# A decoder trunk in split float32: the residual weights' slots moved by 64 bytes, with longer slots and a smaller transfer scratch

## The chip, the cores and the metric

The kernel runs on one core of a Trainium2 chip. A core has a matmul engine (TensorE, PE in the profile; its loads of stationary operands are listed as PEld), VectorE (DVE), ScalarE (ACT), GpSimd (POOL) and SyncE (SP), which issues most transfers between HBM and SBUF, the on-chip memory of 128 partitions. Matmul results go to PSUM banks. The metric is the device time of one execution in microseconds (us); lower is better.

## The reference, cut to what matters

The trunk has two layers on 256 positions of width 2048. Each layer has a token mixer (forgetting attention in the first, sliding-window attention in the second) and a gated feed-forward block with a short convolution; all operands are float32.

```python
for i in range(DEPTH):
    mod = c_act @ ada_w[i] + ada_b[i]
    sh1, sc1, g1, sh2, sc2, g2 = jnp.split(mod[:, None, :], 6, axis=-1)
    h = x * (1.0 + sc1) + sh1
    ...
    x = layer_norm(DEEPNORM_ALPHA * x + (1.0 + g1) * y, ln_mix_g[i], ln_mix_b[i])
    h = x * (1.0 + sc2) + sh2
    y = conv_ffn(h, ffn_w_up[i], ffn_conv_w[i], ffn_conv_b[i], ffn_w_down[i])
    x = layer_norm(DEEPNORM_ALPHA * x + (1.0 + g2) * y, ln_ffn_g[i], ln_ffn_b[i])
```

The mixers' projections, the up projection (2048 to 11264) and the down projection (5632 to 2048) are the large products. Weights are read once each, 256 positions wide.

## The kernel before, in words

**Split operands.** TensorE multiplies in the type float32r, a rounded float32. To keep precision, each operand is split in two: a rounded part (h, "high") and a residual (l, "low"), which is the operand minus its rounded part. A product is then three matmuls: high by high, high by low, low by high. For weights the function `stream` does this, a block at a time: a transfer (L261) brings 256 rows by 512 columns of a weight matrix into a slot `w` as 128 partitions x 2 x 512 elements, ScalarE rounds it into `wh` (L264), and VectorE subtracts, `wl = w - wh` (L275, in `residual_`, which is placed in the program some steps ahead of use). Then `go` runs the matmuls that use the pair. There are 728 such blocks.

**Three ways to use a block.** In `w_mm` (outputs named ws in the profile) and `u_mm` (us) a 128 x 128 slice of the weights is the stationary operand and the activations `hHL` are streamed; hHL holds for each block of 128 features 256 high and then 256 low elements. `u_mm`, the up projection, alternates: stationary slice of wh, 512 columns streamed (high and low together); stationary slice of wl, 256 columns streamed (high alone). `w_mm` uses 256 columns each: wh with high, wh with low, wl with high. In `x_mm` (outputs xs) it is the other way about: the activations are stationary, 128 positions at a time, and 512 columns of wh or wl are streamed, in the order wh by high, wl by high, wh by low. The stationary operand is then hHL (value projection of the first mixer, projections of the second), `oT` (attention output, in both output projections; the last four of its sixteen blocks are kept in hHL's place) or `gT` (down projection). All these matmuls are recorded at L75, in the helper `mm`. A stationary operand is loaded while the matmul before it still streams, as the starts in the PEld rows show.

**Memory.** Tiles come from pools of slots of equal length, one set for each tag; a slot starts at a multiple of 32 bytes. `wp` has ten slots of 4,096 bytes (tag w, also used for the modulation weights wa and others), `hl` four slots for wh and four for wl, each of 4,096 bytes, and `gp` thirty slots of 2,048 bytes (gT, oT, and others). In front of all pools lies a scratch for transfers issued by POOL, 4,096 bytes a partition, set in `kernel` (L1179). In the allocation of the program a partition has, from its first byte on:

```text
scratch        0     hHL      27904     w (10 slots)   78816
x           6912     acc      62080     wh (4 slots)  119776
                                        wl (4 slots)  136160
                                        gp (30 slots) 152544
                                        end           229256
```

Modulo 128 this makes 0 for hHL and 96 for w, wh, wl and gp, in every slot.

**Order.** The tile framework orders instructions and places the waits. SP issues the transfers of weights (w and wa), in program order. POOL issues small ones: rows of parameters (L146 to L175) and the bias row of a gate (L392), 1 MB broadcast to all partitions. VectorE also accumulates the modulation vectors (L404), one step of which `tick` adds after each block. Between sublayers the layer norm runs: moments on VectorE (L636 to L641), the power of -1/2 on POOL (L642), normalising on ScalarE and VectorE (L652, L654), transposes on TensorE (L493) and the split into hHL.

Of the kernel before, what the change touches and what calls it, by code (L numbers as in the profile page):

```python
# [11 lines left out]
F32R = mybir.dt.float32r  # L12
# [5 lines left out]
P = 128  # L18
# [18 lines left out]
WB = 512  # L37
# [4 lines left out]
def hybrid_trunk(ctx: ExitStack, tc: tile.TileContext, a: dict, out: bass.AP):  # L42
    nc = tc.nc
# [6 lines left out]
    hl = ctx.enter_context(tc.tile_pool(name="hl", bufs=4))  # L50
# [4 lines left out]

    def wtile(name="w"):
        return wp.tile([P, 2, WB], F32, tag="w", name=name)

    def gtile(name="g"):
        return gp.tile([P, 2, S], F32R, tag="g", name=name)  # L60
# [16 lines left out]
    def pin(ins, on=True):  # L77

        if on:
            tc.keep_in_program_order(ins)  # L80
# [140 lines left out]
    def settle(left=0):  # L221
        while work and (ahead[0] > left or not left):
            f = work.pop(0)
            rest(f, *work)
            f()
# [21 lines left out]
    def run_post():  # L247
        for g in list(post):
            if next(g, post) is post:
                post.remove(g)  # L250
# [5 lines left out]
    def stream(wsrc, row0, col, ks, use):  # L256

        for kc in ks[::2]:
            r0 = (row0 + kc) * P
            w = wtile()  # L260
            pin(nc.sync.dma_start(w, wsrc[r0:r0 + 2 * P, col:col + WB].rearrange("(k p) f -> p k f", p=P)), False)  # L261
            h = hl.tile([P, 2, WB], F32R, tag="wh", name="wh")
            l = hl.tile([P, 2, WB], F32R, tag="wl", name="wl")
            pin(nc.scalar.copy(h, w), False)  # L264

            def go(kc=kc, h=h, l=l):
                ahead[0] -= 1
                run_post()
                use(kc, h, l)
                if feeds:  # L270
                    feeds.pop(0)()
                tick()

            def residual_(w=w, h=h, l=l, go=go):
                pin(nc.vector.tensor_tensor(l, w, f32(h), op=ALU.subtract), behind[0] > 0)  # L275
                behind[0] -= 1
                del residuals[go]

            ahead[0] += 1
            weights.add(go)  # L280
            residuals[go] = residual_
            work.append(go)
            settle(2)
# [46 lines left out]
    def x_stationary(wsrc, col, k0, nk, stat, end=0):  # L330

        ps = x_banks()
        use = x_mm_end(ps, stat, nk, end) if end else lambda kc, h, l: x_mm(ps, kc, h, l, stat, nk - 1)
        stream(wsrc, k0, col, list(range(nk)), use)
        return ps

    def w_stationary(wsrc, col):

        ps = u_banks()
        stream(wsrc, 0, col, list(range(KC)), lambda kc, h, l: u_mm(ps, kc, h, l))  # L340
        return ps
# [24 lines left out]
    def tick():  # L366
        ada_tick()
        if not feeds:
            step()
# [10 lines left out]
    def ada_vector(l, v):  # L380
# [14 lines left out]
        for k in range(KC):  # L395
            for c in range(0, D, D // 2):
                w = wtile("wa").rearrange("p a f -> p (a f)")
                pin(nc.sync.dma_start(w, a["ada_w"][l, k * P:(k + 1) * P, v * D + c:v * D + c + D // 2]), False)
                for o in range(0, D // 2, step_):
                    ac, wo = part(c + o, step_), w[:, o:o + step_]  # L400
                    if k == 0 and not row:
                        pin(nc.vector.tensor_scalar_mul(ac, wo, cact[:, 0:1]), True)
                    else:
                        pin(nc.vector.scalar_tensor_tensor(ac, wo, (cactp if row else cact)[:, k:k + 1], ac,  # L404
                                                           op0=ALU.mult, op1=ALU.add), True)
                yield
# [249 lines left out]
    def ln_rows(name, l):  # L656
        gb, bb = [], []
        for c in range(0, D, D // 2):
            for b, nm in ((gb, "_g"), (bb, "_b")):
                w = wtile("ln")  # L660
                nc.sync.dma_start(w.rearrange("p a f -> p (a f)"), a[name + nm][l, c:c + D // 2].partition_broadcast(P))
                b += [w[:, 0, :], w[:, 1, :]]
        return gb, bb
# [78 lines left out]
    def out_proj(oT, full, w_o, l):  # L742
        def stat(kc, t):
            while kc not in full:
                step()
            return oT[kc][0][:, t * P:(t + 1) * P], oT[kc][1][:, t * P:(t + 1) * P]

        ps = {d: x_banks() for d in range(2)}

        def part(d, ks):  # L750
            use = x_mm_end(ps[d], stat, KC, 2) if d == D // WB - 1 else                 lambda kc, h, l_: x_mm(ps[d], kc, h, l_, stat, KC - 1)
            stream(w_o, 0, d * WB, ks, use)

        for i, ks in enumerate((range(0, 8), range(8, 12))):
            then(lambda i=i: ada.update(rate=((1.3, 1.3, 1.3, 1.3), (0.9,) * 4)[l][i]))
            for d in range(2):
                part(d, list(ks))
        then(lambda: ada_need(l, 2))
        for d in range(D // WB):
            if d < 2:  # L760
                part(d, list(range(12, KC)))
            else:
                then(lambda d=d: ada.update(rate=((1.3, 1.3, 1.3, 1.3), (0.9,) * 4)[l][d]))
                ps[d] = x_banks()
                part(d, list(range(KC)))
            then(lambda d=d: defer(residual(ps[d], d, gates[l, 2], True)), d == D // WB - 1)
        then(lambda: (flush(), ada.update(gate_free=True)), True)
# [423 lines left out]
```

## Time and profile before

| | |
|---|---|
| median of 3 runs | 2251.49 us (2250.17 to 2252.9) |
| the profiled execution | 2256.46 us |
| its span, first to last instruction | 2254.7 us |
| mean granted TensorE clock | 0.990 |
| matmuls | 12087 |
| moved from and to HBM | 602.66 MB |

A row of a group names line, engine, operation, output tile and inputs, shapes and a count, then the group's busy time, the mean duration of one in ns, and the idle time of the engine just before its instructions, with what ended it. The duration of a matmul includes its way through the array, so one that follows on the heels of another overlaps it: the distance from start to start is shorter than the duration. In a timeline row the first two numbers are start and length in us; neighbouring instructions of one form are merged, with their count behind the x.

### The profile page before, as it was taken

The page shows a single profiled execution, that of the slowest core. Times are in us where ns is not written, and L with a number is a line of the kernel's source. Part 1 is how long each engine was busy: PE and PEld are TensorE (multiplying, and loading weights), DVE is VectorE, ACT ScalarE, POOL GpSimd, SP SyncE. Part 2 cuts the span into 40 slices and gives each one's busy share as a digit, 9 for nine tenths or more (in the row PEclk, how much of TensorE's full clock was granted, in tenths as well). Part 3 has the DMA queues.
Part 4 walks back from the last instruction along what each step waited for, and adds up shares of the span by engine and source line. Part 5 has one row for each costly group of instructions (what it writes and reads, how often), then busy time and mean ns, then how long its engine had stood idle before and what let it go on. Part 6 is the DMA issues. An engine that isn't in the chain of part 4 may idle for free. (4 is left out here: it accounts for less than half of the span.)

```text
span 2254.7 us, 33120 instructions
## 1 busy us (share of the span) xinstructions
PE 2203.7 (98%) x12087; PEld 1908.6 (85%) x12087; DVE 1847.5 (82%) x2626; ACT 1209.7 (54%) x2009; POOL 22.8 (1%) x52
## 2 busy tenths in 40 slices
PE   6999999999999999999999999999999999999997
PEld 5999888788888888888887788788888888888886
DVE  6879999979989978799888899769988655676766
ACT  3435655455555543655634588746555533555542
POOL 0000000000000000000000000000000000000000
PEclk9999999999999999999999999999999999999999
DMA  9999999958978989889887777557887555565553
GB/s 336 371 336 364 349 357 325 329 200 298 327 266 296 315 299 339 272 277 319 280 309 284 244 246 243 206 185 262 289 270 256 190 192 195 189 193 189 188 195 112
DMA packets 274228, 602.66 MB, mean 267 GB/s; under 512 B 21062, under 2 KB 29960, under 8 KB 273552
## 3 DMA queue, kind: packets, MB, share of 16 engines
q1 hardware_dynamic: 273008, 595.85, 76.5%
q0 software_dynamic: 1056, 4.69, 0.6%
q8 instruction: 94, 1.54, 0.3%
q14 instruction: 70, 0.57, 0.1%
HBM read 598.37 MB, written 2.10 MB: 266 GB/s over the span
## 5 line engine op out<-in xcount | busy, mean ns | idle before, releaser
L264 ACT CAST wh<-w 128x1024 fp32r<-128x1024 f32 x728 | 763.8, 1051 | 806.4 <-PE us L75 284.5
L275 DVE TENSOR_TENSOR wl<-w,wh 128x1024 fp32r<-128x1024 f32 x728 | 887.2, 1223 | 297.0 <-ACT wh L264 285.1
L75 PE MATMUL us<-hHL,wh 128*128 128x512 f32 x2816 | 983.7, 393 | 0.0
L75 PE MATMUL us<-hHL,wl 128*128 128x256 f32 x2816 | 790.4, 282 | 3.0 <-DVE wl L275 3.0
L75 PEld LDWEIGHTS us<-hHL,wh 128*128 128x128 f32 x2816 | 528.9, 188 | 112.0 <-issue 2.5
L75 PEld LDWEIGHTS us<-hHL,wl 128*128 128x128 f32 x2816 | 533.0, 189 | 8.4 <-DVE wl L275 4.3
L75 PE MATMUL xs<-wh,gT 128*128 128x512 f32 x1408 | 435.5, 390 | 0.0
L75 PEld LDWEIGHTS xs<-wh,gT 128*128 128x128 f32 x1408 | 264.3, 188 | 54.6
L75 PE MATMUL xs<-wl,gT 128*128 128x512 f32 x704 | 273.9, 389 | 0.0
L75 PE MATMUL xs<-wh,hHL 128*128 128x512 f32 x704 | 237.6, 403 | 0.1
L404 DVE SCALAR_TENSOR_TENSOR acc<-wa,cact,acc 128x1024 f32<-128x1024 f32 x180 | 228.8, 1280 | 0.0
L75 PE MATMUL ws<-hHL,wh 128*128 128x256 f32 x1024 | 191.3, 289 | 4.4 <-ACT hHL L84 2.1
L75 PEld LDWEIGHTS ws<-hHL,wh 128*128 128x128 f32 x1024 | 163.1, 196 | 6.9 <-ACT hHL L84 2.3
L404 DVE SCALAR_TENSOR_TENSOR acc<-wa,cactp,acc 128x1024 f32<-128x1024 f32 x128 | 162.6, 1281 | 0.0
L75 PEld LDWEIGHTS xs<-wh,hHL 128*128 128x128 f32 x704 | 131.5, 189 | 29.4 <-issue 1.0
L75 PEld LDWEIGHTS xs<-wl,gT 128*128 128x128 f32 x704 | 132.2, 188 | 27.3
L75 PE MATMUL ws<-hHL,wl 128*128 128x256 f32 x512 | 144.7, 290 | 2.2 <-DVE wl L275 2.2
L75 PE MATMUL xs<-wl,hHL 128*128 128x512 f32 x352 | 140.6, 400 | 1.6 <-DVE wl L275 1.5
L75 PE MATMUL xs<-wh,oT 128*128 128x512 f32 x384 | 124.6, 394 | 0.8 <-ACT wh L264 0.7
L1075 ACT ACTIVATE u<-us,ccol 128x256 f32<-128x256 f32 x176 | 98.0, 561 | 39.6 <-DVE us L1073 39.5
L75 PEld LDWEIGHTS ws<-hHL,wl 128*128 128x128 f32 x512 | 99.5, 197 | 2.8 <-DVE wl L275 2.8
L1076 DVE SCALAR_TENSOR_TENSOR u<-us,ccol,u 128x255 f32<-128x255 f32 x176 | 83.6, 480 | 13.2 <-ACT u L1075 12.9
(222 smaller groups left out, 1761.2 us busy)
## 6 DMA issues: line engine op xcount, KB each, us to landing
w<-in_ffn_w_up_dram SPq DMA_DIRECT2D x352, 512.0 KB, 4.6
wa<-in_ada_w_dram SPq DMA_DIRECT2D x320, 512.0 KB, 5.4
w<-in_ffn_w_down_dram SPq DMA_DIRECT2D x176, 512.0 KB, 4.1
w<-in_fox_w_in_dram SPq DMA_DIRECT2D x96, 512.0 KB, 7.0
wo<-in_ada_w_dram SPq DMA_DIRECT2D x48, 512.0 KB, 8.4
w<-in_swa_w_in_dram SPq DMA_DIRECT2D x40, 512.0 KB, 5.0
w<-in_fox_w_o_dram SPq DMA_DIRECT2D x32, 512.0 KB, 6.2
w<-in_swa_w_o_dram SPq DMA_DIRECT2D x32, 512.0 KB, 4.7
```

Of the source, the lines that this page charges most:

```text
L75: return nc.tensor.matmul(o, lhsT, rhs, start=start, stop=stop, **kw)
L264: pin(nc.scalar.copy(h, w), False)
L275: pin(nc.vector.tensor_tensor(l, w, f32(h), op=ALU.subtract), behind[0] > 0)
L404: pin(nc.vector.scalar_tensor_tensor(ac, wo, (cactp if row else cact)[:, k:k + 1], ac, op0=ALU.mult, op1=ALU.add), True)
L1075: nc.scalar.activation(u, pf, AF.Identity, bias=cw(CW, f), scale=cw(2, f))
L1076: nc.vector.scalar_tensor_tensor(u[:, 1:], pf[:, :S - 1], cw(1, f), u[:, 1:], op0=ALU.mult, op1=ALU.add)
```

## The change

The slots of wh and wl become 128 bytes longer (32 elements), 4,224 in place of 4,096 bytes. The tile wh starts at the beginning of its slot as before, wl 64 bytes (16 elements) into its slot. The scratch for POOL's transfers becomes 2,048 in place of 4,096 bytes. No instruction is named, added or taken away by the diff.

```diff
+    def htile(name):
+        o = 16 * (name == "wl")
+        return hl.tile([P, 2 * WB + 32], F32R, tag=name, name=name)[:, o:o + 2 * WB].rearrange("p (k f) -> p k f", f=WB)
...
-            h = hl.tile([P, 2, WB], F32R, tag="wh", name="wh")
-            l = hl.tile([P, 2, WB], F32R, tag="wl", name="wl")
+            h, l = htile("wh"), htile("wl")
...
-    nc = _bacc.Bacc("TRN2", target_bir_lowering=False, num_devices=1, dynamic_dma_scratch_size=4096)
+    nc = _bacc.Bacc("TRN2", target_bir_lowering=False, num_devices=1, dynamic_dma_scratch_size=2048)
```

## The prediction

> **What bounds the kernel now.** I read the page first: busy times, then the clock row.
>
> ```profile
> span 2254.7 us, 33120 instructions
> PE 2203.7 (98%) x12087; PEld 1908.6 (85%) x12087; DVE 1847.5 (82%) x2626; ACT 1209.7 (54%) x2009; POOL 22.8 (1%) x52
> PEclk9999999999999999999999999999999999999999
> ```
>
> TensorE is without a matmul for only 2254.7 - 2203.7 = 51 us, at a granted clock of 0.9 or more in every slice. A busy matmul engine can still run slower than it might, so the question is how far apart matmuls start. The second view is the page's costliest groups:
>
> ```profile
> L264 ACT CAST wh<-w 128x1024 fp32r<-128x1024 f32 x728 | 763.8, 1051 | 806.4 <-PE us L75 284.5
> L275 DVE TENSOR_TENSOR wl<-w,wh 128x1024 fp32r<-128x1024 f32 x728 | 887.2, 1223 | 297.0 <-ACT wh L264 285.1
> L75 PE MATMUL us<-hHL,wh 128*128 128x512 f32 x2816 | 983.7, 393 | 0.0
> L75 PE MATMUL us<-hHL,wl 128*128 128x256 f32 x2816 | 790.4, 282 | 3.0 <-DVE wl L275 3.0
> ...
> L75 PE MATMUL xs<-wl,gT 128*128 128x512 f32 x704 | 273.9, 389 | 0.0
> ...
> L75 PE MATMUL ws<-hHL,wl 128*128 128x256 f32 x512 | 144.7, 290 | 2.2 <-DVE wl L275 2.2
> L75 PE MATMUL xs<-wl,hHL 128*128 128x512 f32 x352 | 140.6, 400 | 1.6 <-DVE wl L275 1.5
> ```
>
> The rounding on ScalarE (L264) waits mostly for TensorE to free a slot, and the subtraction on VectorE (L275) waits mostly for ScalarE: both are ahead of the matmuls. The list of TensorE's waits says the same. All its waits for a residual add up to 3.0 + 2.3 + 2.2 = 7.5 us:
>
> ```profile
> PE us L75 <- DVE wl L275: 3.0, 3, 1.4
> PE xs L75 <- DVE wl L275: 2.3, 4, 0.8
> PE ws L75 <- DVE wl L275: 2.2, 2, 1.4
> ```
>
> So the end is set by the rate at which matmuls follow each other. A change that leaves every instruction in place can act through that rate, or through a new stall of TensorE.
>
> Is the rate the same wherever operands lie? The third view, TensorE's timeline where the output projection passes from stationary operands in the gp pool (named oT) to ones in hHL, answers that. Line, columns, moving operands and clock are the same on both sides:
>
> ```profile
> 464.07 0.39 PE L75 MATMUL xs<-wl,oT 128*128 128x512 f32 x1
> 464.29 0.61 PE L75 MATMUL xs<-wh,oT 128*128 128x512 f32 x2
> ...
> 466.11 0.39 PE L75 MATMUL xs<-wl,oT 128*128 128x512 f32 x1
> ...
> 466.80 0.39 PE L75 MATMUL xs<-wl,hHL 128*128 128x512 f32 x1
> 467.03 0.63 PE L75 MATMUL xs<-wh,hHL 128*128 128x512 f32 x2
> ...
> 468.20 0.40 PE L75 MATMUL xs<-wl,hHL 128*128 128x512 f32 x1
> ```
>
> From 464.07 to 466.11 there are three groups of three matmuls: 2.04 us / 9 = 226.7 ns from start to start. From 466.80 to 468.20 there are two groups: 1.40 / 6 = 233.3 ns. Nothing but the stationary operand's place differs, and it costs 6.6 ns a matmul, 3%. The durations of the groups in single stretches (TensorE, forms kept apart) give the same step without counting, and a third case, the up projection from 1600 to 1750 us:
>
> ```profile
> L75 PE MATMUL xs<-wl,oT 128*128 128x512 f32 x23 | 9.0, 389 | 0.0
> ...
> L75 PE MATMUL xs<-wl,hHL 128*128 128x512 f32 x8 | 3.2, 395 | 0.0
> ...
> L75 PE MATMUL us<-hHL,wh 128*128 128x512 f32 x432 | 150.3, 391 | 0.0
> ```
>
> So three classes of 512-column matmul are seen: 389, 391 and 395 ns. The page's 393, 390 and 400 are means with stalls in them, so I price by the stretches. I set beside the classes the first byte of each operand, modulo 128, from the allocation told in the section on the kernel: hHL starts at 0, and w, wh, wl and all of gp at 96. Tile sizes and slices are multiples of 512 bytes, so the remainder holds within a tile. "Distance" means the start of the streamed operand minus that of the stationary one loaded during the stream:
>
> - xs with gp stationary: 96 - 96, distance 0: 389 ns
> - us, hHL streamed while a slice of wl is loaded: 0 - 96, which is 32 modulo 128: 391 ns
> - xs with hHL stationary: 96 - 0, distance 96: 395 ns
>
> **The change part by part.** It adds and removes no instruction. All of SBUF moves down by 2,048 bytes, and what lies behind hl up again by 8 x 128 = 1,024; both are multiples of 128, so every remainder stays, but for one: wl goes from 96 to 96 + 64 = 160, which is 32.
>
> *Slots of wl, up projection.* Each of the 2816 us matmuls on wh streams hHL (at 0) while a slice of wl (now at 32) is loaded: distance 0 - 32, which is 96. That is the class of hHL as stationary, 395 instead of 391: 2816 x 4 ns = +11.3 us. With rounded means, 3 to 5 ns: +8.4 to +14.1. The 2816 matmuls on wl stream hHL while wh is loaded, whose remainder is kept: 0.
>
> *ws.* 512 slices of wl are loaded during a 256-column stream of hHL, with the same move from 32 to 96. No row shows 256 columns at distance 96. It lies between 0 and the 4 ns of 512 columns, 0 to +2.0 us; I take half, for half the columns: +1.0.
>
> *xs, gp stationary.* Besides the 704 on gT there are these on oT:
>
> ```profile
> L75 PE MATMUL xs<-wl,oT 128*128 128x512 f32 x192 | 75.1, 391 | 0.8 <-DVE wl L275 0.8
> ```
>
> Together 704 + 192 = 896 matmuls stream wl at 32 against 96: distance 64, which the trace does not have. Nearest are 389 (what it was) and 395; below, nothing excludes one more step of 6: -6 to +6 ns, -5.4 to +5.4 us. I take the middle between the two seen neighbours, 392: 896 x 3 = +2.7. *xs, hHL stationary:* 352 matmuls go from distance 96 to 32, 395 to 391: -1.4.
>
> *Longer slots of wh.* Slots 4,224 bytes apart keep their remainder modulo 128 and change it modulo 256 and 512. Before, slots were 4,096 apart, so within a class all distances differ by multiples of 512 only, and the trace cannot say whether such a longer period matters. Bound: the step of 6 ns, either way, on three of four slots of the 2816 + 3744 matmuls of 512 columns (in xs each matmul on wl comes with two on wh: 3 x (704 + 192 + 352) = 3744): 6560 x 0.75 x 6 = 29.5 us. I take 0, since no row asks for it.
>
> *VectorE and ScalarE.* L275 reads w and wh and writes wl; before, all three have one remainder, afterwards wl has another. If sharing it cost time, shorter subtractions with other remainders would be cheaper per element. They aren't:
>
> ```profile
> L85 DVE TENSOR_TENSOR hHL<-t,hHL 128x512 fp32r<-128x512 f32 x25 | 17.2, 688 | 1.4 <-ACT hHL L84 1.3
> ...
> L85 DVE TENSOR_TENSOR gT<-u,gT 128x256 fp32r<-128x256 f32 x88 | 37.0, 420 | 2.4 <-ACT gT L84 1.9
> ```
>
> From 256 to 512 elements (a write to gp at 96, then one to hHL at 0) the step is 268 ns, from 512 to 1024 (L275) it is 535: the same 1.05 ns an element. So 0; were 1223 to change by 5% (61 ns x 728 = 45 us of VectorE), the 297 us of VectorE's idle time ahead of L275 cover it. Without that cover the residual would be late, and behind it every matmul on wl.
>
> *Scratch.* It serves the transfers that POOL issues, 4.69 MB in all:
>
> ```profile
> q0 software_dynamic: 1056, 4.69, 0.6%
> ```
>
> On POOL only one kind of request has urgent work right behind it, that for the gate's bias row (L392), ahead of the layer norm's pow (L642):
>
> ```profile
> 260.22 0.56 POOL L392 DMA_DIRECT2D acc<-in_ada_b_dram  x1 [49.87 <-DVE wl L275]
> ...
> 476.09 0.60 POOL L392 DMA_DIRECT2D acc<-in_ada_b_dram  x1 [3.24 <-PE sm L75]
> 476.71 0.57 POOL L642 TENSOR_TENSOR rs<-mv,mhalf 128x1 f32<-128x1 f32 x1
> ...
> 1501.53 0.58 POOL L392 DMA_DIRECT2D acc<-in_ada_b_dram  x1 [3.30 <-DVE cv L428]
> ```
>
> Were POOL held in that request, rs would be late, then the normalised x, the transposes and the first matmuls of the up projection. I take 0: the transfer before on that queue is from 260.22 us, long landed. The other end is a full landing at both places, with the page's row of issues:
>
> ```profile
> acc<-in_ada_b_dram POOLq DMA_DIRECT2D x4, 1024.0 KB, 6.2
> ```
>
> 2 x 6.2 = 12.4 us.
>
> *Sum:* 11.3 + 1.0 + 2.7 - 1.4 = +13.6 us. The profiled execution took 2256.5 us (span 2254.7 and 1.8 around it), so it becomes 2270.1; it lies 5.0 above the median of 2251.5, and by the median the changed kernel takes **2265 us**. The terms' own bounds give 8.4 + 0 - 5.4 - 1.8 = +1 to 14.1 + 2.0 + 5.4 - 1.1 = +20 us, 2253 to 2272.
>
> A rule of the Trainium skill speaks against all of this. Its page "TensorE: Matmul & The Clock Gate", in "Part 2: What happens when you issue a matmul", gives TensorE separate read ports for streamed and stationary operands and says: "Loading the next tile's weights doesn't steal SBUF read bandwidth from the running matmul." By it the places of the two should not matter, and the sum would be 0. The rows at 464 and 467 us disagree by 6.6 ns a matmul.
>
> **The rivals.**
>
> *No effect (2251 to 2252 us).* The step between gp and hHL may come from something that 64 bytes don't touch: hHL lies below byte 61,000 of a partition and gp above 152,000, or only the remainder modulo 64 counts, which stays 32 for wl. For it: one comparison with hHL carries my reading. Against: us streams from the same hHL and comes out near the gp class. The Trainium skill has this rival as a rule: its page "SBUF — State Buffer", in "Who interferes with whom", ends by saying that TensorE and ScalarE never wait on anyone.
>
> *Faster: only the stationary operand's own remainder counts.* 0 gives 395, 96 gives 389 and 391, and 32, never tried, may lie as far on the other side of 96. The place is the loading of wl's slices in the up projection: 2816 x 6 ns = -16.9 us, 2235 us; the xs terms vanish, since there wl is streamed. It decides from the point where wl's new place costs less than 391 in the us rows. For it: the two classes at 96 differ by 2 ns although their streams start at 0 and at 96, so the stream seems to matter little. Against: it needs a remainder better than any seen. Gains through the longer slots would show in the same way, up to the 29.5 us above.
>
> *Slower through POOL:* up to +12.4, 2264, from the point where a request waits for room.
>
> **How the numbers follow.** Forecast (the distance counts) 0.45, faster rival 0.36, no effect 0.15, POOL 0.04. Both first cases exceed 0.2% (4.5 us, about what a measurement of this kernel can tell from no change) but for their edges: faster 0.37, same 0.16, slower 0.47. The likeliest case alone gives 2253 to 2272. Holding 8 in 10 needs the faster rival with some gain through the longer slots at the bottom, 2228, and forecast plus about half of that bound's loss at the top, 2280.
>
> **What would show it.** Right: 512-column us rows near 395 in an undisturbed stretch, xs rows on wl with hHL near 391, every other class as before, and L275, L264 and TensorE's idle time unchanged. The distance reading is wrong if us stays at 391 (no effect) or falls below it (faster). The term for distance 64 is read from the xs rows on wl with gT, against those on wh in the same stretch; if the rows on wh move too, the longer slots act. A pow later than 1 us after its request shows POOL. All fails if the order of instructions changes.

## The result, and the profile after

The changed kernel takes 2273.19 us (median of 3 runs, 2271.89 to 2274.74) against 2251.49: 1.0097 times as long, with a 95% interval of 1.0074 to 1.012. The forecast was 2265. The profiled execution took 2271.89 us. Its page has these rows; the helper `mm` is now at L79, the rounding at L267, the subtraction at L278.

```profile
span 2270.1 us, 33120 instructions
PE 2221.5 (98%) x12087; PEld 1902.8 (84%) x12087; DVE 1848.7 (81%) x2626; ACT 1207.7 (53%) x2009; POOL 25.4 (1%) x52
PEclk9999999999999999999999999999999999999999
L267 ACT CAST wh<-w 128x1024 fp32r<-128x1024 f32 x728 | 762.0, 1048 | 831.3 <-PE us L79 300.0
L278 DVE TENSOR_TENSOR wl<-w,wh 128x1024 fp32r<-128x1024 f32 x728 | 887.3, 1223 | 312.1 <-ACT wh L267 300.6
L79 PE MATMUL us<-hHL,wh 128*128 128x512 f32 x2816 | 991.8, 397 | 0.0
L79 PE MATMUL us<-hHL,wl 128*128 128x256 f32 x2816 | 785.6, 281 | 3.0 <-DVE wl L278 3.0
...
L79 PE MATMUL xs<-wh,gT 128*128 128x512 f32 x1408 | 442.2, 394 | 0.0
...
L79 PE MATMUL xs<-wl,gT 128*128 128x512 f32 x704 | 276.5, 393 | 0.0
...
L79 PE MATMUL xs<-wl,hHL 128*128 128x512 f32 x352 | 140.6, 400 | 1.2 <-DVE wl L278 1.0
```

Nothing waits longer. TensorE is without a matmul for 2270.1 - 2221.5 = 48.6 us (51 before), the clock row is the same, the subtraction takes 1223 ns as before, and the number of instructions is the same. Every engine also carries them out in the same order, in this and in all the kernels below. The matmuls follow each other more slowly, and not only those that touch wl: the rows of wh on gT had been these on the page of before:

```profile
L75 PE MATMUL xs<-wh,gT 128*128 128x512 f32 x1408 | 435.5, 390 | 0.0
```

A duration contains an overlap, so I read the pace from the starts. In TensorE's timeline of the changed kernel, five groups of three matmuls on gT lie between these two rows:

```profile
1840.18 0.39 PE L79 MATMUL xs<-wl,gT 128*128 128x512 f32 x1
...
1843.63 0.40 PE L79 MATMUL xs<-wl,gT 128*128 128x512 f32 x1
```

That is 3.45 us / 15 = 230.0 ns a matmul. The same view of the kernel before, again over five groups:

```profile
1840.01 0.39 PE L75 MATMUL xs<-wl,gT 128*128 128x512 f32 x1
...
1843.40 0.39 PE L75 MATMUL xs<-wl,gT 128*128 128x512 f32 x1
```

Here it is 3.39 / 15 = 226.0. Taken over the whole trace, as the mean distance between the recorded starts of successive matmuls on wl within a run of them, divided by three and with pauses left out, it is 231.2 against 226.8. In the same way the pair of the up projection (512 columns on wh, 256 on wl) goes from 346.7 to 349.7 ns. These paces come near the loss: 2816 pairs x 3.0 = 8.4 us, 2112 matmuls on gT x 4.4 = 9.3, 576 on oT x 3.4 = 2.0, 512 groups of ws x 2.3 = 1.2, and xs on hHL -0.4: 20.5 us (20.6 before rounding), with 21.7 measured between the medians. The two profiled executions, from which the paces are read, differ by only 15.4 us, for the one of before took 5.0 more than its median and the one of after 1.3 less. Added up over all intervals between starts, pauses included, the up projection takes 8.0 us longer in the trace of after, xs on gT 9.3, and xs on oT and hHL together 1.3, but ws takes 1.7 us less. So the loss of the up projection and of xs on gT is seen both ways, and the term of ws is not clear of its pauses.

The list of TensorE's waits shows no new stall either:

```profile
PE us L79 <- DVE wl L278: 3.0, 3, 1.4
PE xs L79 <- DVE wl L278: 1.5, 3, 0.6
PE ws L79 <- DVE wl L278: 2.2, 2, 1.4
```

On POOL the pow follows the request for the gate's row by 0.02 us, as before:

```profile
473.99 0.60 POOL L395 DMA_DIRECT2D acc<-in_ada_b_dram  x1 [3.24 <-PE sm L79]
474.61 0.57 POOL L645 TENSOR_TENSOR rs<-mv,mhalf 128x1 f32<-128x1 f32 x1
```

### The profile page after: what moved, and what is told of

Read it like the earlier page. It is cut to its first block, busy times and chain, and to the rows that moved or that the text cites. A ratio compares the mean times of both kernels' runs of the same rounds, so it can differ in the third digit from the quotient of the medians.

```text
span 2270.1 us, 33120 instructions
## 1 busy us (share of the span) xinstructions
PE 2221.5 (98%) x12087; PEld 1902.8 (84%) x12087; DVE 1848.7 (81%) x2626; ACT 1207.7 (53%) x2009; POOL 25.4 (1%) x52
## 3 DMA queue, kind: packets, MB, share of 16 engines
q0 software_dynamic: 1056, 4.69, 0.6%
## 5 line engine op out<-in xcount | busy, mean ns | idle before, releaser
L267 ACT CAST wh<-w 128x1024 fp32r<-128x1024 f32 x728 | 762.0, 1048 | 831.3 <-PE us L79 300.0
L278 DVE TENSOR_TENSOR wl<-w,wh 128x1024 fp32r<-128x1024 f32 x728 | 887.3, 1223 | 312.1 <-ACT wh L267 300.6
L79 PE MATMUL us<-hHL,wh 128*128 128x512 f32 x2816 | 991.8, 397 | 0.0
L79 PE MATMUL us<-hHL,wl 128*128 128x256 f32 x2816 | 785.6, 281 | 3.0 <-DVE wl L278 3.0
L79 PEld LDWEIGHTS us<-hHL,wh 128*128 128x128 f32 x2816 | 529.2, 188 | 125.0 <-issue 2.5
L79 PEld LDWEIGHTS us<-hHL,wl 128*128 128x128 f32 x2816 | 530.2, 188 | 8.4 <-DVE wl L278 4.3
L79 PE MATMUL xs<-wh,gT 128*128 128x512 f32 x1408 | 442.2, 394 | 0.0
L79 PEld LDWEIGHTS xs<-wh,gT 128*128 128x128 f32 x1408 | 264.5, 188 | 60.8
L79 PE MATMUL xs<-wl,gT 128*128 128x512 f32 x704 | 276.5, 393 | 0.0
L79 PE MATMUL xs<-wh,hHL 128*128 128x512 f32 x704 | 238.1, 404 | 0.1
L79 PE MATMUL ws<-hHL,wh 128*128 128x256 f32 x1024 | 191.0, 289 | 4.4 <-ACT hHL L88 2.1
L79 PEld LDWEIGHTS ws<-hHL,wh 128*128 128x128 f32 x1024 | 162.5, 195 | 6.9 <-ACT hHL L88 2.3
L79 PEld LDWEIGHTS xs<-wl,gT 128*128 128x128 f32 x704 | 132.3, 188 | 30.1
L79 PEld LDWEIGHTS xs<-wh,hHL 128*128 128x128 f32 x704 | 131.7, 189 | 29.2 <-issue 1.0
L79 PE MATMUL ws<-hHL,wl 128*128 128x256 f32 x512 | 144.2, 289 | 2.2 <-DVE wl L278 2.2
L79 PE MATMUL xs<-wl,hHL 128*128 128x512 f32 x352 | 140.6, 400 | 1.2 <-DVE wl L278 1.0
L79 PE MATMUL xs<-wh,oT 128*128 128x512 f32 x384 | 125.9, 398 | 0.8 <-ACT wh L267 0.7
L79 PEld LDWEIGHTS ws<-hHL,wl 128*128 128x128 f32 x512 | 98.5, 195 | 2.9 <-DVE wl L278 2.8
L1079 DVE SCALAR_TENSOR_TENSOR u<-us,ccol,u 128x255 f32<-128x255 f32 x176 | 83.6, 480 | 14.7 <-ACT u L1078 14.6
```

What stands on the lines that cost most here:

```text
L79: return nc.tensor.matmul(o, lhsT, rhs, start=start, stop=stop, **kw)
L1079: nc.vector.scalar_tensor_tensor(u[:, 1:], pf[:, :S - 1], cw(1, f), u[:, 1:], op0=ALU.mult, op1=ALU.add)
```

## The experiments

All kernels differ from the kernel before in addresses alone. Times are medians beside runs of the kernel before on the same chip (2255.1, 2254.0 and 2254.4 us in the three sets of timed runs). The columns of starts are means over the whole trace, found as above; the last column adds the change of all these paces times their counts (us, xs on gT, on oT and on hHL, ws).

| kernel | time, us | ratio (95%) | us pair, ns | xs on gT, ns | xs on hHL, ns | sum by starts, us |
|---|---|---|---|---|---|---|
| before | 2251.49 | | 346.7 | 226.8 | 233.9 | |
| changed | 2273.19 | 1.0097 (1.0074 to 1.012) | 349.7 | 231.2 | 233.5 | +20.6 |
| changed, again (e9) | 2273.88 | 1.0089 (1.0075 to 1.0103) | 349.7 | 231.2 | 233.8 | +20.8 |
| scratch alone (e1) | 2254.54 | 0.9997 (0.9988 to 1.0006) | 346.7 | 226.8 | 233.8 | -0.1 |
| slots + 128 alone (e2) | 2266.45 | 1.0050 (1.0037 to 1.0062) | 348.0 | 230.6 | 233.9 | +14.0 |
| slots + 256 alone (e5) | 2252.8 | 0.9995 (0.9986 to 1.0004) | 346.7 | 226.8 | 234.0 | +0.1 |
| wl + 64 alone (e3) | 2282.67 | 1.0116 (1.0101 to 1.0132) | 352.1 | 232.0 | 233.4 | +28.9 |
| wl + 128 alone (e6) | 2267.8 | 1.0063 (1.005 to 1.0076) | 346.8 | 232.8 | 233.6 | +17.4 |
| all against hHL: distance 0 (e4) | 2262.76 | 1.0039 (1.0026 to 1.0052) | 351.6 | 226.8 | 229.8 | +13.8 |
| distance 16 (e10) | 2259.75 | 1.0024 (1.0014 to 1.0033) | 349.5 | 226.8 | 231.3 | +5.7 |
| distance 48 (e11) | 2263.18 | 1.0038 (1.0025 to 1.005) | 350.0 | 226.8 | 231.3 | +9.9 |
| distance 64 (e8) | 2269.48 | 1.0062 (1.0049 to 1.0074) | 353.3 | 226.8 | 230.4 | +12.7 |
| distance 96 (e7) | 2266.68 | 1.0054 (1.0041 to 1.0067) | 351.2 | 226.8 | 234.0 | +14.7 |

"Distance" in the last five rows is the start of hHL minus that of w, wh, wl and gp, modulo 128; in the kernel before it is 32. For each kernel the sum by starts lies within 7 us of the measured difference, and within 4 for all but e4.

### Taking the change apart

**Scratch alone (e1).** The kernel before, with this edit:

```diff
-    nc = _bacc.Bacc("TRN2", target_bir_lowering=False, num_devices=1, dynamic_dma_scratch_size=4096)
+    nc = _bacc.Bacc("TRN2", target_bir_lowering=False, num_devices=1, dynamic_dma_scratch_size=2048)
```

> The scratch alone halved, slots as before. Both theories of the address, the distance modulo 128 (D) and longer periods through the longer slots (L): no change, within 5 us of the kernel before, all groups of matmuls as before. The POOL rival: up to 12 us slower, with the pow late behind the bias row's request.

The ratio is 0.9997 (0.9988 to 1.0006). The row of the up projection in TensorE's groups stays within 1 ns:

```profile
L75 PE MATMUL us<-hHL,wh 128*128 128x512 f32 x2816 | 982.0, 392 | 0.0
```

So half the scratch costs nothing here, and the rival on POOL falls.

**Longer slots alone (e2).** The changed kernel with both tiles at the start of their slots:

```diff
-        o = 16 * (name == "wl")
+        o = 0
```

> Slots of 4,224 bytes and half the scratch, wl at the beginning of its slot. D (only the distance modulo 128 counts): no change, xs on gT at 389 ns and us on wh at 391 ns. L (remainders of a longer period count, and slots 4,096 apart kept them equal): xs on wh with gT at 394 ns as in the changed kernel, 8 us or more of the loss; the us rows tell whether their loss belongs to the 64 bytes or to the slots.

It takes 1.0050 (1.0037 to 1.0062). The groups on TensorE:

```profile
L79 PE MATMUL us<-hHL,wh 128*128 128x512 f32 x2816 | 987.6, 395 | 0.0
...
L79 PE MATMUL xs<-wh,gT 128*128 128x512 f32 x1408 | 441.1, 393 | 0.0
...
L79 PE MATMUL xs<-wl,gT 128*128 128x512 f32 x704 | 275.9, 392 | 0.0
```

Every remainder modulo 128 is that of the kernel before, and yet xs on gT rises from 390 and 389 to 393 and 392, on wh as on wl. The longer slots thus cost 11 us by themselves (2266.45 - 2255.11). A remainder modulo 128 can't be all that counts. Nor can the distance between the two streamed tiles: a block's wh and wl lie 16,896 bytes apart here, a multiple of 512 as before. What changes from slot to slot, modulo 256, is their distance to the stationary gT.

**wl moved by 64 bytes alone (e3).** Slots of 4,096 bytes again, the scratch of 2,048; wl gets a pool of its own behind a tile of 64 bytes, and 448 bytes behind it keep gp's remainder modulo 512.

```diff
+    pad1 = ctx.enter_context(tc.tile_pool(name="pad1", bufs=1))
+    hl2 = ctx.enter_context(tc.tile_pool(name="hl2", bufs=4))
+    pad2 = ctx.enter_context(tc.tile_pool(name="pad2", bufs=1))
...
+            l = hl2.tile([P, 2, WB], F32R, tag="wl", name="wl")
...
+    pad1.tile([P, 16], F32, name="pad1")
+    pad2.tile([P, 112], F32, name="pad2")
```

> wl 64 bytes further by one pad between the slots of wh and those of wl, all slots 4,096 apart, gp moved by multiples of 512 bytes, half the scratch. D: +10 to +14 us, us on wh at 395 ns, xs on wl with gT at 389 to 393, xs on wh with gT at 389. L: us on wh between 391 and 395, xs on wh with gT at 389; the loss of xs on wh is gone. If the stationary operand's remainder alone counts: us as under D, xs on wl unchanged.

```profile
L78 PE MATMUL us<-hHL,wh 128*128 128x512 f32 x2816 | 997.6, 398 | 0.0
L78 PE MATMUL us<-hHL,wl 128*128 128x256 f32 x2816 | 788.9, 282 | 3.0 <-DVE wl L278 3.0
L78 PE MATMUL xs<-wh,gT 128*128 128x512 f32 x1408 | 442.9, 394 | 0.0
L78 PE MATMUL xs<-wl,gT 128*128 128x512 f32 x704 | 277.1, 394 | 0.0
```

This is the slowest layout of all, 1.0116 (1.0101 to 1.0132), against 1.0089 (1.0075 to 1.0103) for the whole change (e9). These intervals touch, and the two were timed on different chips, but the paces of the traces agree: 352.1 against 349.7 ns for the pair, 232.0 against 231.2 on gT. The two parts don't add: e2 and e3 together would cost 38.9 us, and the change cost 21.7. With the longer slots, 64 bytes cost less than without them. In xs the matmuls on wh slow down as much as those on wl, though wh and gT lie as before relative to each other, modulo 512. A matmul's pace therefore depends on its neighbours in the sequence also.

Other engines' accesses at the same time aren't the reason. Sorted by what ran when they started, and without pauses, matmuls on gT follow each other in this kernel after 232.0 ns with and 232.0 without a subtraction on VectorE (L278), after 232.1 with and 231.9 without a rounding on ScalarE (L267), and after 232.0 both with at most two and with more than eight packets of transfers under way. In the kernel before, it is 226.8 in each of these cases. Nor do the loads of stationary operands take longer as the profile records them. The rows of those loaded for the matmuls on wl, first in the kernel before, then in this one:

```profile
L75 PEld LDWEIGHTS xs<-wl,gT 128*128 128x128 f32 x704 | 132.2, 188 | 27.3
```

```profile
L78 PEld LDWEIGHTS xs<-wl,gT 128*128 128x128 f32 x704 | 132.1, 188 | 31.0
```

A load takes 188 ns in both; what grows, by 3.7 us / 704 = 5.3 ns for each, is the idle time before them.

**Slots longer by 256 bytes (e5).**

```diff
-        o = 16 * (name == "wl")
-        return hl.tile([P, 2 * WB + 32], F32R, tag=name, name=name)[:, o:o + 2 * WB].rearrange("p (k f) -> p k f", f=WB)
+        o = 0
+        return hl.tile([P, 2 * WB + 64], F32R, tag=name, name=name)[:, o:o + 2 * WB].rearrange("p (k f) -> p k f", f=WB)
```

> Slots of wh and wl longer by 256 bytes (4,352), wl at the beginning of its slot, half the scratch. Theory P256 (TensorE's two reads, streamed operand and stationary operand being loaded, disturb each other by their distance modulo 256): no change, below 2 us, xs on gT at 389 ns. P512 (modulo 512): slower as with slots longer by 128, about 11 us, xs on gT near 393. Theory of other engines' writes into neighbouring slots: also slower than before, since the slots no longer lie a power of two apart.

```profile
L79 PE MATMUL us<-hHL,wh 128*128 128x512 f32 x2816 | 982.9, 393 | 0.6 <-DVE acc L407 0.6
...
L79 PE MATMUL xs<-wh,gT 128*128 128x512 f32 x1408 | 435.7, 390 | 0.0
```

Each mean is that of the kernel before, and the ratio 0.9995 (0.9986 to 1.0004). 128 bytes more between slots matter and 256 don't, as if what counts repeated every 256 bytes; no other multiple of 256 was tried in this place.

**wl moved by 128 bytes (e6).** As e3, with 128 bytes ahead of wl and 384 behind.

```diff
-    pad1.tile([P, 16], F32, name="pad1")
-    pad2.tile([P, 112], F32, name="pad2")
+    pad1.tile([P, 32], F32, name="pad1")
+    pad2.tile([P, 96], F32, name="pad2")
```

> wl 128 bytes further by one pad, all slots 4,096 apart, gp as it was modulo 512, half the scratch. P256: slower, since 128 is half a period: xs on wl with gT above 389, and xs on wh in the same sequence with it. If 128 were a period (the prediction's reading D): no change.

```profile
L78 PE MATMUL us<-hHL,wh 128*128 128x512 f32 x2816 | 982.9, 394 | 0.2 <-ACT wh L267 0.2
...
L78 PE MATMUL xs<-wh,gT 128*128 128x512 f32 x1408 | 443.5, 395 | 0.0
...
L78 PE MATMUL xs<-wl,gT 128*128 128x512 f32 x704 | 277.6, 394 | 0.0
```

The up projection keeps its pace (346.8 ns), xs on gT loses a little more than in e3 (232.8 against 232.0 ns). So 128 is no period for xs. For us it looks like one here, but in e2, where every remainder modulo 128 stays too, the pair rose to 348.0 ns.

### Moving hHL against everything else

**Distances 0, 64 and 96 (e4, e8, e7).** A small tile behind hHL moves w, wh, wl and gp together, by 32, 96 and 64 bytes (e7 and e8 with the scratch of 2,048).

```diff
+    cst.tile([P, 8], F32, name="pad")
```

> The kernel before with 32 unused bytes behind hHL, so that w, wh, wl and gp start at 0 modulo 128, as hHL does; slots, offset and scratch as before. D: all distances are 0, all 512-column groups go to 389 ns: us 2816 x -2 and xs on hHL 1056 x -6, -12 us. If the stationary operand's remainder alone counts (0 is the bad one): us and xs on gp go to 395, about +27 us. If neither counts (the region of the partition): no change.

```profile
L75 PE MATMUL us<-hHL,wh 128*128 128x512 f32 x2816 | 996.0, 400 | 0.0
L75 PE MATMUL us<-hHL,wl 128*128 128x256 f32 x2816 | 784.5, 280 | 3.1 <-DVE wl L275 3.1
L75 PE MATMUL xs<-wh,gT 128*128 128x512 f32 x1408 | 435.6, 390 | 0.0
...
L75 PE MATMUL xs<-wh,hHL 128*128 128x512 f32 x704 | 235.4, 400 | 0.1
```

> 96 unused bytes behind hHL: w, wh, wl and gp start at 64 modulo 512, half the scratch; distance to hHL 64 and -64 modulo 256. P256: xs on gT at 389, us and xs on hHL as they come; a sum of the us pair below 346 ns or xs on hHL below 229 start to start would make it faster than the kernel before.

> 64 unused bytes behind hHL: w, wh, wl and gp start at 32 modulo 128 (all at 32 modulo 512), hHL at 256 as before; half the scratch. Only distances to hHL change, to 32 and -32 modulo 256. P256: xs on gT stays at 389 ns, us and xs on hHL move; by the prediction's classes us on wh would take 395 and xs on hHL 391. If the stationary operand's own remainder counts: xs on gT moves too.

The group of us on wh and that of xs on hHL in e8:

```profile
L75 PE MATMUL us<-hHL,wh 128*128 128x512 f32 x2816 | 1000.4, 400 | 0.0
...
L75 PE MATMUL xs<-wh,hHL 128*128 128x512 f32 x704 | 235.4, 400 | 0.0
```

In e4 the distance is 0 everywhere, the remainder at which xs on gT has its best pace, and the up projection is slower all the same, 400 ns; by the prediction's classes this kernel would have gained 12 us, and it lost 7.7. In e7 us on wh rose to 398 ns, but xs on hHL stayed within 1 ns of before, 402 on wh and 400 on wl, where the classes asked for a fall of 4. In all of these kernels xs on gT keeps 226.8 ns, whatever its operands' own remainders are (0, 32, 64, 96): relative places count, places by themselves don't. That takes away, for xs, the rival that the stationary operand's own remainder decides. xs on hHL gains up to 4 ns a matmul (233.9 to 229.8 in e4), but there are only 1056 of them.

**Distances 16 and 48 (e10, e11).** hHL starts 16 bytes into a longer tile, which also moves what follows, by 32 and by 128 bytes; scratch of 2,048.

```diff
-    hHL = cst.tile([P, KC, 2, S], F32R, name="hHL")
+    hHL = cst.tile([P, KC * 2 * S + 8], F32R, name="hHL")[:, 4:4 + KC * 2 * S]
+    hHL = hHL.rearrange("p (k a s) -> p k a s", a=2, s=S)
```

> hHL 16 bytes into a tile 32 bytes longer, half the scratch: w, wh, wl and gp at 0 modulo 512, hHL at 16 modulo 128, so the up projection runs at distance 16 modulo 128, between the classes 0 (351 ns for a pair of us matmuls, start to start) and 32 (347 ns, the kernel before). If 32 is the best place: +0 to +13 us, xs on gT unchanged at 389. If a place between is better: us pairs below 346 ns and a kernel faster than before.

> hHL 16 bytes into a tile 128 bytes longer, half the scratch: the up projection at distance 48 modulo 128, between the classes 32 (347 ns a pair) and 64 (353 ns). If 32 is the best place: 0 to +18 us, xs on gT unchanged. If a place between is better: us pairs below 346 ns and faster than before.

They take 1.0024 and 1.0038. No distance tried gives a faster kernel than 32, where the kernel before stands; among these five kernels a stretch with a mean pair below 346 ns appears only in e10 (345.4 ns from 525 to 575 us). In e11 the slices of wl start at 96 modulo 128 as in the kernel before, and the pair takes 350.0 ns: for the up projection, too, the stationary operand's own remainder modulo 128 doesn't decide.

### One layout, two paces

**The changed kernel again (e9).**

> The changed kernel once more, beside the next two on one chip: P256 makes no new claim, it should come out 17 to 27 us above the kernel before, the interval first measured; the point is whether its loss lies below that of the 64 bytes alone (1.16%).

It repeats the first result: 2273.88 us, 19.5 above the kernel before, and the same paces.

**e7 once more (e12).** The paces in the table are means, and in e3, e4, e7 and e10 they hide two levels. The starts show the up projection of e7 holding 353 ns a pair for a long stretch and 347 in another, with the same addresses. Its groups on TensorE from 1575 to 1675 us and from 2000 to 2100 us:

```profile
L75 PE MATMUL us<-hHL,wh 128*128 128x512 f32 x284 | 100.4, 397 | 0.0
```

```profile
L75 PE MATMUL us<-hHL,wh 128*128 128x512 f32 x290 | 100.6, 392 | 0.0
```

Six more fit into the same 100 us of the second. The kernel was run once more to see whether that comes back:

> The kernel of the run shifted by 64 bytes, unchanged, profiled once more. In its first profile the up projection kept one pace per stretch, with the same addresses in all of them: from start to start of a pair (512 and 256 columns) 353 ns from 500 to 770 us, 347 ns from 875 to 950 us, 353 ns from 975 to 1120 us, 353 ns from 1500 to 1790 us and 347 ns from 1925 to 2150 us. If addresses and the order of work alone pick the pace, the same stretches show the same paces again, 347 ns from 1925 to 2150 us among them. If it is picked by the moment at which a stretch happens to begin, at least one of the stretches shows the other pace (347 in place of 353 or the reverse), and the row of us on wh over the whole span leaves 398 ns by 1 ns or more.

It took 2266.7 us, with 2253.84 for the kernel before beside it (one run each). The same two windows:

```profile
L75 PE MATMUL us<-hHL,wh 128*128 128x512 f32 x284 | 100.4, 397 | 0.0
```

```profile
L75 PE MATMUL us<-hHL,wh 128*128 128x512 f32 x290 | 100.6, 392 | 0.0
```

The counts and means are the same, and every stretch named in the expectation shows its pace again, 347 from 1925 us on included. In these two profiles chance doesn't pick the level; something that comes with the place in the program does, beside the addresses. e10 has the widest case: 347 ns for most of its up projections, but from 950 to 1120 us the pace of these rows of its timeline, seven pairs in 2.52 us, 360 ns each:

```profile
949.96 0.28 PE L75 MATMUL us<-hHL,wl 128*128 128x256 f32 x1
...
952.48 0.28 PE L75 MATMUL us<-hHL,wl 128*128 128x256 f32 x1
```

## Why the prediction held, and where it did not

**What bounds the kernel: held.** With no wait and no instruction added, TensorE's busy time rose by 17.8 us and the span by 15.4. The loss is in the rate of matmuls, as forecast. The time lies in the range of 2228 to 2280 us, but 1 us above the 2253 to 2272 of the likeliest case alone.

**us on wh, +11.3 us: held in kind, a little too large.** The row rose by 4 ns as forecast (393 to 397), but the row on wl, forecast unchanged, fell by 1 (282 to 281), and the matmul behind it starts 1 ns sooner. The pair lost 3.0 ns from start to start, 8.4 us. Pricing by the duration of one half of an alternating pair was the slip. The sign that the prediction named, us near 395 ns in an undisturbed stretch, came: from 1600 to 1750 us, where it had been 391,

```profile
L79 PE MATMUL us<-hHL,wh 128*128 128x512 f32 x431 | 150.6, 394 | 0.0
```

**xs on wl with gp stationary, +2.7 us: the term that failed.** The forecast was 392 ns for the rows on wl and no change for those on wh. Both moved, to 393 and 394 on gT. It costs 9.3 us on gT and 2.0 on oT. Two steps failed together. "I take 0, since no row asks for it", for the longer slots, was wrong: they alone cost 11 us (e2), inside the bound of 29.5 that was given. And the price of a moved operand isn't paid by its own matmuls alone: with wl moved and the slots as they were (e3), those on wh pay as much. So the sign named for the longer slots, that the rows on wh move too, doesn't tell the two apart.

**"Distance" modulo 128: falls as a rule.** It counted right that relative places matter and that 64 bytes slow the up projection. But the remainder modulo 128 doesn't name the pace: e2 and e6 change xs without changing it, e4 has distance 0 and a slow up projection, and e7 has two paces at one distance. That the forecast came near is partly luck: for 64 bytes alone the same steps give +13.6, against 27.6 measured (2282.67 - 2255.11), and the longer slots, put at 0, cost 11 alone; that the two together cost only 21.7 was not foreseen.

**xs on wl with hHL stationary, -1.4 us; ws, +1.0 us.** By starts -0.4 for all of xs on hHL, and +1.2 for ws, or -1.7 with its pauses counted, so that neither size nor sign of ws is shown. The duration of xs on wl with hHL didn't go to 391: 400 before and after.

**VectorE, ScalarE, scratch, POOL: 0, held** (1223 ns unchanged; rounding 1051 to 1048; e1).

**The rivals.** No effect falls by e3, e7 and e8, each in the same regions of memory as before and slower by 0.5 to 1.2%. With it falls, for this kernel, what the Trainium skill says on its pages "TensorE: Matmul & The Clock Gate" (Part 2: What happens when you issue a matmul) and "SBUF — State Buffer" (Who interferes with whom), as far as one would conclude from them that the places of the two operands don't matter: moving them costs up to 6.6 ns a pair in e8. TensorE's waits on other engines did not grow. The runs don't show that the read of one takes bandwidth from the other; they show that their relative start is part of the pace. The faster rival falls by the result itself, 21.7 us the other way, and by e11; the rival on POOL by e1 and by the pow, which follows its request by 0.02 us.

**Open.** Why a remainder is good or bad, how a matmul's operands reach the pace of its neighbours, what sets the level at the start of a stretch, and why the longer slots soften the 64 bytes. The traces record when a load or a matmul starts, not how TensorE reads its operands.

## What to carry to other kernels

Where TensorE has no idle time left, read its pace from start to start, over a whole group of alternating matmuls, before believing that a change of layout is free: here no wait, no count and no order changed, and 1% went. A move of one tile is to be tried by itself and together with the others, since its price did not follow from the tile's own matmuls; of the changes to the slots and to single tiles, only slots 256 bytes longer kept every pace. When memory is rearranged around a kernel whose layout no trial beats, as here, pad so that the remainders modulo 256 stay.

## What the runs showed of the hardware

- In long stretches the pair of the up projection holds one of a few mean levels in the kernel before and in those that only move hHL against the rest (e4, e7, e8, e10, e11): 346.7, 350.0, 353.3 or 360.0 ns, which are 104, 105, 106 and 108 times 3.33 ns. One layout can have two of them, each for more than 100 us, and two profiles of e7 agreed on which stretch has which. With slots 128 bytes longer the pairs are mixed, and the means lie between: 349.4 to 349.7 ns in stretches of the changed kernel.
- A matmul whose own operands keep their places relative to each other, modulo 512, can lose 4 to 5 ns because its neighbour's were moved (xs on wh with gT, 390 to 394 in e3 and 395 in e6).
- 128 bytes more in a slot cost more than the work of VectorE, ScalarE and the transfers in the same memory, which costs a running matmul nothing that can be seen (226.8 ns with and without each of them in the kernel before).
